# One core, a diffusion block with 16 experts: expert weights loaded in pairs of units, the last down matrix by column blocks, residual gates spread by transposes

## The chip, the cores and the metric

The kernel runs on one core of one Trainium2 chip, in fp32. The metric is the device time of one execution in microseconds (us), shown as the median of three runs. One of its executions was profiled; its rows are read further down.

## The reference

What is computed, cut to what matters here (512 latent tokens and 256 context tokens of 1024 channels, one layer):

```python
def ec_moe(h, w_r, w_g, w_u, w_d):
    cap = EC_CAPACITY_FACTOR * l_ // N_EXPERTS        # 64 tokens for each of 16 experts
    affinity = jax.nn.softmax((h @ w_r).astype(jnp.float32), axis=-1)
    gate, idx = lax.top_k(jnp.swapaxes(affinity, 1, 2), cap)
    xs = jax.vmap(lambda hb, ib: hb[ib])(h, idx)
    hid = jax.nn.silu(jnp.einsum('becd,edf->becf', xs, w_g)) * jnp.einsum('becd,edf->becf', xs, w_u)
    ye = jnp.einsum('becf,efd->becd', hid, w_d) * gate[..., None].astype(h.dtype)
...
        sh1, sc1, gt1, sh2, sc2, gt2 = adaln(c, w_ada[layer], b_ada[layer])
...
        h_lat = modulate(rms_norm(x, g_mix[layer]), sh1, sc1)
        u_l, q_l, v_l, gf_l, gb_l, g_l = split_proj(h_lat @ w_in[layer], lb)
...
        mix_l = jnp.concatenate([fourier_mix(u_l, w_fourier[layer]), rec_l], axis=-1) @ w_out[layer]
        x = x + gt1 * mix_l
...
        x = x + gt2 * ec_moe(modulate(rms_norm(x, g_ffn[layer]), sh2, sc2), w_router[layer],
                             w_exp_gate[layer], w_exp_up[layer], w_exp_down[layer])
    return rms_norm(x, g_final)
```

The experts' inner width is 2816. Their weights (gate, up and down, 16 x 3 x 1024 x 2816 floats) are 553 MB, nearly all that the kernel reads.

## The kernel before, in words

**Front.** The modulation vectors (shift, scale and residual gate, "ada") are a product of one row with `w_ada`. The class `AdaGroup` makes the last 4 x 1024 of them in two groups: `step` loads 1 MB of `w_ada` (L378, on SP) and VectorE multiplies and adds (L383, L385); `finish` adds over partitions on TensorE (L398), adds the bias on VectorE (`adag`, L400) and transposes (`adagT`, L403). Both `brow`, the bias, and `adag` live in two buffers with the tag `gcc`, which the function `ctx_states` takes over right behind for the scan states of the context (memset on POOL, L544; scans on DVE, L549 and L551; transposes on PE, L558). The residual gates `gt1b` and `gt2b` are the same row on every partition: a broadcast DMA reads the one partition row of `adag` 128 times (64 times), from ACT's queue, L589 and L615, two DMAs each.

Around this the input projection runs in segments of 512 columns (`ff`, `fb`, `v`, `g`, `u`, four steps each): a step's weights (512 KB, `fb1r` for step 1 of `fb`, L133, on SP) are split in a high part by ACT (`fb1wh`, L304) and a low part by POOL (`fb1wl`, L309), and TensorE multiplies three times (L145 to L147). The order of instructions on PE, DVE, ACT, POOL and SP is written by hand there (a manual schedule), and each engine works its list off in order. The gates of a finished segment go through ACT (L526, L532) and DVE. Then come heads, Fourier part, output projection and routing, a chain of computation up to about 370 us.

**Experts.** A matrix comes in 8 units of 128 x 2816 floats (1408 KB), one DMA each, all on SP's queue. Units lie in a ring of 13 equal areas: `slot()` names the next, `load_slot` (L1349) loads a unit in it when the area's last reader is done, and `load_ahead` (L1354) loads the first 13, and a fourteenth, `first`, in the memory of the hidden rows. A unit of the gate and up matrices is 128 rows of 11264 B that follow one another in memory; of the down matrix it is 128 runs of 11264 B that lie 45056 B apart. TensorE takes the units one by one: `up()` for gate (g) and up (u) (L1403), then `dn` (L1455); then `cb` (L1464) adds the expert's rows to `acc_x` on DVE (L1467). A DMA also needs one of eight completion lanes: a DMA waits for the one eight before it.

**The last expert** goes down in five column blocks (three of 256 columns, two of 128). `down_last` loads them by 22 DMAs (L1496) with runs of 1024 B or 512 B, and multiplies (`dq`, L1500); `combine_last` adds and normalises (`cq`, L1516), and out go four DMAs.

Of the kernel before, what the change touches and what calls it, by code (L numbers as in the profile page):

```python
# [30 lines left out]
NSLOT_L = 7  # L31
NSLOT_R = 6
# [19 lines left out]
# columns of the packed small operands  # L52
# [8 lines left out]
# and of its matrices  # L61
# [4 lines left out]
# columns of the packed shape constants  # L66
# [16 lines left out]
def hybrid_kernel(ctx: ExitStack, tc, x, ctxt, small, const, pos, w_ada, b_ada, w_in, w_out,  # L83
                  wg, wu, wd, out):
# [12 lines left out]
    # ------------------------------------------------------------------ memory that stays  # L97
# [25 lines left out]
    # ------------------------------------------------------------------ loads, in the order of use  # L123
# [52 lines left out]
    class AdaFirst:  # L176
        """Shift and scale of the mixer for channel blocks 2n and 2n+1."""

        def __init__(self, n):
            self.n = n  # L180
            if n % 2 == 0:
                # the memory of the values and of the context's gates
                w = p1b.tile([P, 2, 4, 256], F32, tag="v", name=f"adaw{n}_v")
                self.w = [w[:, 0], w[:, 1]] + [pc.tile([P, 4, 256], F32, tag=f"fctx{d}", name=f"adaw{n}_{d}")
                                               for d in range(2)]
            else:
                self.w = [wst.tile([P, 4, 256], F32, tag="wh" if t % 2 else "wl", bufs=SB, name=f"adaw{n}_{t}")
                          for t in range(4)]
            for t in range(4):
                # half of the rows of both halves of the sum  # L190
# [92 lines left out]
    # ------------------------------------------------------------------ input projection  # L283
    class Segment:
        """Columns col..col+512 of the projection, four steps of 256 channels each."""
# [10 lines left out]
        def split(self, kk, a, high=None, low=None):  # L296
            """High and low parts of half a tile."""
# [16 lines left out]
        def units(self, kk):  # L314
            """One step, in units of one 128x128 block of weights against all its tokens."""
# [33 lines left out]
            if kk in self.by_bank:  # L349
                # bank after bank: the last finish, and the next's first are needed, one by one  # L350
# [16 lines left out]
    class AdaGroup:  # L367
        """Columns g*2048..(g+1)*2048 of the modulation of the latent stream."""
# [4 lines left out]
        def step(self, k):  # L373
# [6 lines left out]
            # the products per channel of the sum; the tensor engine adds over the partitions  # L380
# [7 lines left out]
        def finish(self):  # L388
# [15 lines left out]
            return row, raw(tp[:], 0, [[32, 4], [P, 4]])  # L404
# [13 lines left out]
    # columns that add the partial sums  # L418
# [88 lines left out]
    # the gates, per head: forward, backward, queries  # L507
# [42 lines left out]
            # minus the decayed keys  # L550
# [72 lines left out]
    class Filler:  # L623
        """Work without close dependences, to be issued between the steps of the heads.

        What waits for a unit's matmuls is issued behind the next unit's.
        """
# [17 lines left out]
        def take(self, n):  # L645
            """Issues units; returns the tensor engine's time, negative where nothing should follow at once."""
# [22 lines left out]
    # the table of the function that the gate needs, loaded ahead  # L669
# [27 lines left out]
    # ------------------------------------------------------------------ HGRN2 heads  # L697
# [8 lines left out]
    def head_init(h):  # L706
        f, q = fq[:, h, 0:2, :], fq[:, h, 2, :]
        # slots: keys forward, queries backward, queries forward, keys backward
# [229 lines left out]
    def after_u():  # L938
        u_sb = p1b.tile([P, NH, S], F32, tag="u", name="u_sb")

        def wo_step(k, n):
# [51 lines left out]
        def positions(g):  # L993
# [10 lines left out]
            def evict():  # L1004
                # positions 0 and 256 of the cosines; even frequencies stand first
# [93 lines left out]
    class Steps:  # L1099
        """A generator with the tensor engine's time of each step."""  # L1100
# [19 lines left out]
    def fill_to(t, n=99):  # L1120
        """Issues units until the tensor engine has t us of work, n at most."""
# [57 lines left out]
    # ------------------------------------------------------------------ routing  # L1179
# [31 lines left out]
    # nothing, above the least, equal to it  # L1211
# [45 lines left out]
    def top(n):  # L1257
        """The CAP largest values of a row of candidates, in order."""
# [364 lines left out]
```

## Time and profile before

| | |
|---|---|
| median of 3 runs | 1672.88 us (1670.42 to 1674.8) |
| span of the profiled execution | 1668.7 us, 4.2 us under the median of the runs |
| PE, DVE, ACT, POOL busy | 92%, 24%, 15%, 10% |
| DMA packets, bytes | 91448, 608.37 MB |
| chain that ended last | DMA 48%, PE 41%, DVE 5%, ACT 2% |

The span runs from the first instruction to the last of the profiled execution; its own time is this span and the little around it, and the median of the runs stands 4.2 us above it. A busy PE share is not one of PE at its peak. The chain is followed back from the last instruction, at each step to what released it.

### The profile page before, as it was taken

How to read it: one execution, taken by the hardware profiler on the slowest of the kernel's cores; microseconds unless marked ns; L12 is line 12 of the kernel's file. 1: busy time of each engine (PE TensorE's matmuls, PEld its weight loads, DVE VectorE, ACT ScalarE, POOL GpSimd, SP SyncE). 2: the span in 40 equal slices, each digit the busy share in tenths (PEclk: the TensorE clock that was granted, in tenths of full speed). 3: DMA queues.
4: the chain of work that ended last, by engine and by line, in shares of the span. 5: the costliest groups of instructions: out<-in, count | busy, mean ns of one | idle time of the engine just before them, and what ended most of it. 6: DMA issues, size and time to landing. Idle time of an engine off the chain costs nothing.

```text
span 1668.7 us, 19918 instructions
## 1 busy us (share of the span) xinstructions
PE 1529.1 (92%) x8519; PEld 753.1 (45%) x8519; DVE 399.8 (24%) x754; ACT 255.9 (15%) x578; POOL 164.8 (10%) x153
## 2 busy tenths in 40 slices
PE   9978998989999999999898989988988899889897
PEld 6766776874443334343433343334333433243335
DVE  4855678370201010201011001100110111011103
ACT  4512456331000001000100010001000100010002
POOL 2623547400000000000000000000000000000002
PEclk9999999999999989999999998999999989999899
DMA  9785211859999999999999999999999999999998
GB/s 346 283 218 136 77 59 58 334 215 357 422 425 423 424 423 423 423 424 423 424 423 424 424 424 424 423 424 424 423 424 423 423 424 423 424 424 423 424 384 257
DMA packets 91448, 608.37 MB, mean 365 GB/s; under 512 B 8152, under 2 KB 30424, under 8 KB 41184
## 3 DMA queue, kind: packets, MB, share of 16 engines
q1 hardware_dynamic: 90480, 605.21, 88.6%
q10 hardware_dynamic: 880, 1.89, 1.5%
q8 instruction: 67, 1.10, 0.3%
q14 instruction: 21, 0.17, 0.0%
HBM read 604.18 MB, written 2.10 MB: 363 GB/s over the span
## 4 chain that ended last, share of the span: by engine, by line
DMA 48%; PE 41%; DVE 5%; ACT 2%; issue 1%; POOL 1%; SPq 0%; POOLq 0%; DVEq 0%; ACTq 0%
DMA uw<-in_wu_dram 18%; DMA gw<-in_wg_dram 15%; DMA dw<-in_wd_dram 12%; PE dn L1455 9%; PE g L1403 7%; PE u L1403 6%; PE gp L1375 4%; PE cb L1464 3%; DMA fb1r<-in_w_in_dram 1%; DMA adabuf<-in_w_ada_dram 1%; ACT xst L1377 1%; DVE X L795 1%; PE op L146 1%; PE op L145 1%; PE op L147 1%
## 5 line engine op out<-in xcount | busy, mean ns | idle before, releaser
L1455 PE MATMUL dn<-dw,hid 128*64 128x512 f32 (+1 forms) x1440 | 315.9, 562 | 9.0 <-DMA dw<-in_wd_dram 9.0
L1403 PE MATMUL u<-uw,xst 128*64 128x512 f32 (+1 forms) x1464 | 298.1, 559 | 23.4 <-DMA uw<-in_wu_dram 23.3
L1403 PE MATMUL g<-gw,xst 128*64 128x512 f32 (+1 forms) x1440 | 300.3, 569 | 0.0
L1403 PEld LDWEIGHTS u<-uw,xst 128*64 128x64 f32 x1464 | 102.7, 137 | 216.0 <-issue 165.1
L1455 PEld LDWEIGHTS dn<-dw,hid 128*64 128x64 f32 x1440 | 113.9, 136 | 168.1 <-issue 126.5
L1403 PEld LDWEIGHTS g<-gw,xst 128*64 128x64 f32 x1440 | 102.7, 139 | 187.0 <-issue 181.6
L1429 DVE TENSOR_TENSOR hid<-u,hid 128x512 f32<-128x512 f32 (+1 forms) x48 | 30.3, 647 | 538.5 <-PE u L1403 522.6
L1464 PE MATMUL cb<-ye,oht 64*128 64x512 f32 x240 | 108.9, 742 | 26.6 <-DVE acc_x L1467 15.6
L1415 ACT ACTIVATE hid<-g 128x512 f32<-128x512 f32 (+1 forms) x48 | 26.7, 561 | 655.2 <-PE g L1403 654.5
L1473 POOL COPY gt2f<-gt2b 64x512 f32<-64x512 f32 x2 | 1.2, 606 | 1265.8 <-DVE hid L1429 1265.8
L1375 PE MATMUL gp<-oh,xn 128*128 128x128 f32 x512 | 84.0, 294 | 23.3 <-ACT xst L1377 23.1
L1375 PEld LDWEIGHTS gp<-oh,xn 128*128 128x128 f32 x512 | 65.0, 190 | 74.5 <-issue 40.0
L1467 DVE TENSOR_TENSOR acc_x<-cb,acc_x 128x512 f32<-128x512 f32 x120 | 78.6, 688 | 57.6 <-PE cb L1464 57.6
L1377 ACT ACTIVATE xst<-gp,sh,a 128x128 f32<-128x128 f32 x64 | 29.3, 457 | 335.2 <-PE gp L1375 178.9
L1464 PEld LDWEIGHTS cb<-ye,oht 64*128 64x128 f32 x240 | 35.3, 206 | 97.2 <-DVE acc_x L1467 73.0
L1459 DVE TENSOR_TENSOR ye<-dn,gt2b 128x512 f32<-128x512 f32 x15 | 10.4, 692 | 214.9 <-PE dn L1455 214.9
L1437 ACT COPY hid<-hT 128x512 f32<-128x512 f32 (+1 forms) x48 | 24.8, 549 | 170.2 <-PE hT L1435 170.2
L1385 DVE TENSOR_TENSOR oh<-iota,posm 128x512 f32<-128x512 f32 x8 | 5.5, 692 | 182.8 <-PE gp L1375 182.7
L385 DVE SCALAR_TENSOR_TENSOR adaacc<-adabuf,cs,adaacc 128x1024 f32<-128x1024 f32 x28 | 44.3, 1642 | 5.1 <-DMA adabuf<-in_w_ada_dram 5.1
L1419 DVE TENSOR_SCALAR ohg<-iota,posm,aff 128x128 f32<-128x128 f32 x64 | 17.9, 343 | 103.2 <-PE ohT L1424 103.2
L1435 PE MATMUL hT<-ident,hid 128*128 128x128 f32 x176 | 29.3, 300 | 7.7 <-DVE hid L1429 5.9
L1435 PEld LDWEIGHTS hT<-ident,hid 128*128 128x128 f32 x176 | 23.9, 212 | 16.0 <-DVE hid L1429 11.6
(602 smaller groups left out, 1530.6 us busy)
## 6 DMA issues: line engine op xcount, KB each, us to landing
uw<-in_wu_dram SPq DMA_DIRECT2D x122, 1408.0 KB, 27.1
dw<-in_wd_dram SPq DMA_DIRECT2D x120, 1408.0 KB, 27.1
gw<-in_wg_dram SPq DMA_DIRECT2D x120, 1408.0 KB, 27.1
adabuf<-in_w_ada_dram SPq DMA_DIRECT2D x16, 1024.0 KB, 6.4
gw0a<-in_wg_dram SPq DMA_DIRECT2D x7, 1408.0 KB, 15.3
uw0a<-in_wu_dram SPq DMA_DIRECT2D x6, 1408.0 KB, 12.3
adaw<-in_w_ada_dram SPq DMA_DIRECT2D x24, 256.0 KB, 7.6
dw<-in_wd_dram SPq DMA_DIRECT2D x6, 768.0 KB, 13.9
```

The lines of the kernel that those rows point to most:

```text
L385: nv.scalar_tensor_tensor(self.acc[:, a], w[:, a], cs[:, k, :1], self.acc[:, a], op0=ALU.mult, op1=ALU.add)
L1375: nt.matmul(gather.gp[:, o:o + P], lhsT=xn[:, i, k * P:(k + 1) * P], rhs=oh[:, i].rearrange("p a j -> p (a j)"), start=(i == 0), stop=(i = ...
L1377: ns.activation(xst[:, k].rearrange("p a j -> p (a j)"), gather.gp[:, o:o + P], AF.Identity, bias=sh2[:, k:k + 1], scale=a2[:, k:k + 1])
L1403: nt.matmul(b[i][64 * hf:64 * hf + 64, :n], lhsT=xst[:, k, e % 2, :], rhs=t[:, hf * HALF + c0:hf * HALF + c0 + n], start=(k == 0), stop=(k ...
L1415: ns.activation(hid[:, c0:c0 + n], gb[i][:, :n], AF.Silu)
L1419: nv.tensor_scalar(ohg[:, i], iota[:, None, :].to_broadcast([P, 2, CAP]), posm[:, i, e:e + 1], aff[:, i, e:e + 1], op0=ALU.is_equal, op1=A ...
L1429: nv.tensor_tensor(hid[:, c0:c0 + n], ub[i][:, :n], hid[:, c0:c0 + n], op=ALU.mult)
L1435: nt.transpose(tp[:, (r - r0) * P:(r - r0 + 1) * P], hid.rearrange("p (f r) -> p r f", r=NROW)[:, r, :], ident)
L1437: ns.copy(hidT[:, r0:r0 + n].rearrange("p r j -> p (r j)"), tp[:, :n * P])
L1455: nt.matmul(db[64 * dh:64 * dh + 64, c0:c0 + n], lhsT=hidT[:, r, 64 * ih:64 * ih + 64], rhs=t[:, o:o + n], start=(ih == 0 and r == 0), sto ...
L1464: nt.matmul(cb, lhsT=oht[hs, i * P:(i + 1) * P], rhs=ye[hs, :], start=True, stop=True, tile_position=(64 * dh, 0))
L1467: nv.tensor_tensor(acc_x[:, i, ds_], cb, acc_x[:, i, ds_], op=ALU.add)
```

## The change

Three parts.

1. **Pairs.** The ring of 13 areas becomes six tiles of two areas each, and one spare area: `area(n)` hands out one area, or two that lie side by side. The table `BURST` says, for each expert's gate, up and down matrix, how many units one DMA loads: for expert 0 and the gate and up matrix of expert 1 single units, on the same 13 areas in the same order as before; from expert 1's down matrix on pairs, which no longer use the spare area. A pair is one DMA of 128 rows of 22528 B. For this the host lays the gate and up matrices out by partition (`wg`, `wu` as [expert, partition, 8 x 2816]), so that a partition's two units follow one another; a partition's row is then 90112 B from the next. The down matrix has its runs side by side already. There are 168 such pairs (4 + 13 x 12 + 8).
2. **Last down matrix.** The host lays it out by column blocks (`wd_last`), so that each of the 22 DMAs has one run per partition, of 6144 B to 1536 B, in place of several of 1024 B or 512 B.
3. **Gates.** The two broadcasts by DMA (L589, L615) go. DVE copies the gate's 8 columns out of `adagT` (`gt1c`, `gt2c`); for each half `spread` makes four transposes of a column that is repeated 128 times (`gt1s`, `gt2s`), which gives the row on every partition in a PSUM bank, and ACT copies it to `gt1b` (`gt2b`).

```diff
-NSLOT_L = 7
-NSLOT_R = 6
+PAIRS_L = 3
+PAIRS_R = 3
+
+BURST = [(1, 1, 1), (1, 1, 2)] + [(2, 2, 2)] * 13 + [(2, 2, 1)]
...
-    arow1, atp = ag1.finish()
+    def spread(cols, j, name):
+        tp = bank("m", name)
+        for i in range(4):
+            nt.transpose(tp[:, i * P:(i + 1) * P], cols[:, 4 * j + i:4 * j + i + 1].to_broadcast([P, P]), ident)
+        return tp
+
+    atp = ag1.finish()
     sh2 = pz.tile([P, NK], F32, name="sh2")
+    gt1c = pc.tile([P, NK], F32, tag="gtc", bufs=2, name="gt1c")
+    nv.tensor_copy(gt1c.rearrange("p (j i) -> p j i", j=2), atp[:, 0:2, :])
     nv.tensor_copy(sh2.rearrange("p (j i) -> p j i", j=2), atp[:, 2:4, :])
     for j in range(2):
-        src = arow1[32 * j:32 * j + 1, :]
-        ns.dma_start(gt1b[:, j * 512:(j + 1) * 512],
-                     bass.AP(src.tensor, src.offset, [list(src.ap[0]), [0, P], [1, 512]]))
+        ns.copy(gt1b[:, j * 512:(j + 1) * 512], spread(gt1c, j, f"gt1s{j}"))
...
     for j in range(2):
-        src = arow2[64 + 32 * j:65 + 32 * j, :]
-        ns.dma_start(gt2b[64 * j:64 * j + 64, :],
-                     bass.AP(src.tensor, src.offset, [list(src.ap[0]), [0, 64], [1, 512]]))
+        ns.copy(gt2b[64 * j:64 * j + 64, :], spread(gt2c, j, f"gt2s{j}")[64 * j:64 * j + 64, :])
...
+    spare = wl_pool.tile([P, DE], F32, name="wl_spare")
+    pairs = [(wl_pool if i < PAIRS_L else wr_pool).tile([P, 2 * DE], F32, name=f"w{i}")
+             for i in range(PAIRS_L + PAIRS_R)]
+    NU = 2 * len(pairs)
+    at, singles = [0], [True]
+    def area(n):
+        if singles[0] and n == 1:
+            u = at[0] % (NU + 1)
+            at[0] += 1
+            return spare if u == 0 else pairs[(u - 1) // 2][:, (u - 1) % 2 * DE:((u - 1) % 2 + 1) * DE]
+        if singles[0]:
+            assert at[0] % (NU + 1) == 0
+            singles[0], at[0] = False, 0
+        u = at[0] % NU
+        assert u % n == 0
+        at[0] += n
+        return pairs[u // 2][:, u % 2 * DE:(u % 2 + n) * DE]
+    def load_unit(w, e, u):
+        key = (w, e, u)
+        if key not in ahead:
+            n = BURST[e]["gud".index(w)]
+            t = area(n)
+            if w == "d":
+                nc.sync.dma_start(t, wds[e, u // 4, :, u % 4 * DE:(u % 4 + n) * DE])
+            else:
+                nc.sync.dma_start(t, {"g": wg, "u": wu}[w][e, :, u * DE:(u + n) * DE])
+            for i in range(n):
+                ahead[w, e, u + i] = t[:, i * DE:(i + 1) * DE]
+        return ahead.pop(key)
...
+            o, src = (ih % nh) * NROW * w, (2 * c0 + ih * w) * NROW
             for r0, r1 in ((0, 4), (4, 8), (8, NROW)) if n == 4 else ((0, 6), (6, NROW)):
-                nc.sync.dma_start(t[:, ih % nh, r0:r1], wdq[:, ih, r0:r1, c0:c0 + w])
+                nc.sync.dma_start(unit[:, o + r0 * w:o + r1 * w], wd_last[:, src + r0 * w:src + r1 * w])
```

Where it moves instructions. On PE, around the first transposes of the modulation (`adagT`), in the third part of segment `ff`, before:

```order
382 L403 MATMUL adagT_962<-ident,adag_955 128x128 x4
383 L146 MATMUL ff_l_747<-hlA,ff3wl 128x512
384 L147 MATMUL ff_l_747<-hlA,ff3wh 128x512
385 L145 MATMUL ff_l_748<-hlA,ff3wh 128x512
386 L146 MATMUL ff_l_748<-hlA,ff3wl 128x512
387 L147 MATMUL ff_l_748<-hlA,ff3wh 128x512
388 L145 MATMUL ff_l_748<-hlA,ff3wh 128x512
```

and of the change:

```order
382 L406 MATMUL adagT_962<-ident,adag_955 128x128 x4
383 L149 MATMUL ff_l_747<-hlA,ff3wl 128x512
384 L150 MATMUL ff_l_747<-hlA,ff3wh 128x512
385 L148 MATMUL ff_l_748<-hlA,ff3wh 128x512
386 L149 MATMUL ff_l_748<-hlA,ff3wl 128x512
387 L150 MATMUL ff_l_748<-hlA,ff3wh 128x512
388 L592 MATMUL gt1s_971<-ident,gt1c 128x128 x4
```

The eight transposes of `gt1s` stand between the matmuls of `ff`, in two lots of four five rows apart; those of `gt2s` stand likewise between the matmuls of `v`.

On SP, in the expert phase, a stretch of expert 2's list before (a unit each; the bracket names the completion lane and the engine that must have read the area):

```order
154 L1349 DMA uw_0_4356<-in_wu_dram 128x2816 [waits DMAHW3_49,PE_49]
155 L1349 DMA uw_1_4364<-in_wu_dram 128x2816 [waits DMAHW4_49,PE_49]
156 L1349 DMA uw_2_4372<-in_wu_dram 128x2816 [waits DMAHW5_49,PE_49]
157 L1349 DMA uw_3_4380<-in_wu_dram 128x2816 [waits DMAHW6_49,PE_49]
158 L1349 DMA uw_4_4388<-in_wu_dram 128x2816 [waits DMAHW7_49,PE_49]
```

and one of the change, a pair each:

```order
144 L1379 DMA w_3673<-in_wg_dram 128x5632 [waits DMAHW7_49,PE_49]
145 L1379 DMA w_3674<-in_wg_dram 128x5632 [waits DMAHW0_49,PE_49]
146 L1379 DMA w_3675<-in_wu_dram 128x5632 [waits DMAHW1_49,PE_49]
147 L1379 DMA w_3676<-in_wu_dram 128x5632 [waits DMAHW2_49,PE_49]
148 L1379 DMA w_3677<-in_wu_dram 128x5632 [waits DMAHW3_49,PE_49]
```

The sequence of matrices is the same, with half the DMAs, each twice as long; six tiles (`w_3673` to `w_3678`) come round.

## Rows read from the trace of the kernel before

**Rows 1.** The page: bytes moved in 40 slices of the span, and the packets.

```profile
GB/s 346 283 218 136 77 59 58 334 215 357 422 425 423 424 423 423 423 424 423 424 423 424 424 424 424 423 424 424 423 424 423 423 424 423 424 424 423 424 384 257
DMA packets 91448, 608.37 MB, mean 365 GB/s; under 512 B 8152, under 2 KB 30424, under 8 KB 41184
```

**Rows 2.** Windows: stretch, length, busy us by engine, PE clock, DMA share, GB/s.

```profile
85.56:93.90 8.34, 8.34 (x50) 7.29 (x48) 7.51 (x4) 0.00 (x0) 5.61 (x3) 1.00 0.46 164
102.00:115.00 13.00, 8.88 (x54) 7.69 (x52) 3.59 (x5) 0.60 (x1) 0.00 (x0) 1.00 0.98 58
103.86:150.20 46.34, 37.75 (x219) 33.43 (x218) 26.18 (x30) 10.10 (x18) 14.32 (x10) 0.93 0.77 209
700.00:1560.00 860.00, 790.90 (x3743) 308.32 (x3741) 99.78 (x177) 53.89 (x106) 0.00 (x0) 0.99 1.01 424
1634.00:1640.00 6.00, 6.00 (x43) 4.02 (x40) 1.38 (x2) 2.04 (x8) 2.39 (x2) 1.00 1.09 349
```

**Rows 3.** The chain that ended last, in order of time: start, length, what.

```profile
720.22 26.00 DMA dw<-in_wd_dram
746.27 27.11 DMA gw<-in_wg_dram
...
1594.24 27.37 DMA uw<-in_wu_dram
```

**Rows 4.** DMA issues: queue, count, KB each, median us from issue to landing.

```profile
uw<-in_wu_dram SPq DMA_DIRECT2D x122, 1408.0 KB, 27.1
dw<-in_wd_dram SPq DMA_DIRECT2D x120, 1408.0 KB, 27.1
...
gt1b<-adag ACTq DMA_DIRECT2D x2, 256.0 KB, 13.3
...
wo3r<-in_w_out_dram SPq DMA_DIRECT2D x1, 512.0 KB, 3.3
```

**Rows 5.** The chain of the stretch 50 to 320 us.

```profile
94.39 23.32 DMA fb1r<-in_w_in_dram
...
153.30 10.69 DMA gt2b<-adag
```

**Rows 6.** Timeline of POOL: start, length, what, and the idle time before.

```profile
117.90 0.10 POOL L544 MEMSET gcc<- 128x2 f32 x1 [21.39 <-DMA gt1b<-adag]
...
164.13 0.10 POOL L544 MEMSET gcc<- 128x2 f32 x1 [11.23 <-DMA gt2b<-adag]
```

**Rows 7.** Timeline of ACT.

```profile
98.51 0.60 ACT L532 ACTIVATE fq<-ff_l 128x512 f32<-128x512 f32 x1 [0.78 <-PE ff_l L147]
```

**Rows 8.** Timeline of PE.

```profile
96.02 0.60 PE L403 MATMUL adagT<-ident,adag 128*128 128x128 f32 x4
...
119.48 0.58 PE L145 MATMUL fb_c<-hctx_h,fb0wh 128*128 128x256 f32 x1 [8.59 <-ACT fctx L526]
...
165.88 0.80 PE L147 MATMUL v_l<-v1wl,hlB 128*128 128x512 f32 x1 [7.53 <-POOL v1wl L309]
```

**Rows 9.** Timeline of DVE.

```profile
153.96 0.14 DVE L610 SCALAR_TENSOR_TENSOR a<-adagT,sm 128x8 f32<-128x8 f32 x1
...
164.09 2.29 DVE L549 TENSOR_TENSOR_SCAN gcc<-fctx,zero 128x255 f32<-128x255 f32 x2 [9.24 <-DMA gt2b<-adag]
```

**Rows 10.** Waits of SP's queue: us in total, times, longest.

```profile
SPq L1349 <- PE g L1403: 164.0, 61, 13.2
```

**Rows 11.** Timeline of SP, then line 1349's DMAs issued from 536 to 552 us.

```profile
522.10 21.68 SPq L1349 DMA_DIRECT2D uw<-in_wu_dram  x6
...
DMA to landing us min/median/max: 12.1/12.6/13.1
```

**Rows 12.** Timeline of PE at expert 2, and at the last u unit.

```profile
536.10 7.31 PE L1403 MATMUL g<-gw,xst 128*64 128x512 f32 x36
...
1621.66 2.58 PE L1403 MATMUL u<-uw,xst 128*64 128x512 f32 x12 [0.81 <-DMA uw<-in_wu_dram]
```

**Rows 13.** Waits of PE: us in total, times, longest.

```profile
PE dq L1500 <- DMA dw<-in_wd_dram: 0.5, 2, 0.3
```

More of the change, by code (lines that the diff above doesn't have):

```diff
@@ L30 @@
 NROW = HALF // P
-NSLOT_L = 7
-NSLOT_R = 6
+PAIRS_L = 3
+PAIRS_R = 3
+BURST = [(1, 1, 1), (1, 1, 2)] + [(2, 2, 2)] * 13 + [(2, 2, 1)]
+BLOCKS = ((0, 256), (256, 256), (512, 256), (768, 128), (896, 128))
 ADA_AT = (1, 4)
@@ L83, in hybrid_kernel @@
 def hybrid_kernel(ctx: ExitStack, tc, x, ctxt, small, const, pos, w_ada, b_ada, w_in, w_out,
-                  wg, wu, wd, out):
+                  wg, wu, wd, wd_last, out):
     nc = tc.nc
@@ L403, in finish @@
                 nt.transpose(tp[:, i * P:(i + 1) * P], row[:, i * P:(i + 1) * P], ident)
-            return row, raw(tp[:], 0, [[32, 4], [P, 4]])
+            return raw(tp[:], 0, [[32, 4], [P, 4]])
     sq = Segment("q", 512, False, False)
@@ L607, in hybrid_kernel @@
         pass
-    arow2, atp = ag2.finish()
+    atp = ag2.finish()
     a2 = pz.tile([P, NK], F32, name="a2")
+    gt2c = pc.tile([P, NK], F32, tag="gtc", bufs=2, name="gt2c")
+    nv.tensor_copy(gt2c.rearrange("p (j i) -> p j i", j=2), atp[:, 2:4, :])
     nv.scalar_tensor_tensor(a2.rearrange("p (j i) -> p j i", j=2), atp[:, 0:2, :], 1.0,
@@ L1332, in hybrid_kernel @@
     wr_pool = tc.alloc_tile_pool(name="wr", bufs=1, side="right", reuse_waits="tile")
-    nslot = NSLOT_L + NSLOT_R
-    cnt = [0]
-    def slot(name):
-        i = cnt[0] % nslot
-        cnt[0] += 1
-        return (wl_pool if i < NSLOT_L else wr_pool).tile([P, DE], F32, tag=f"w{i}", name=name)
-    ahead = {}
-    def load_slot(src, name):
-        if name in ahead:
-            return ahead.pop(name)
-        t = slot(name)
-        nc.sync.dma_start(t, src)
-        return t
-    def load_ahead(w, nm, k, t=None):
-        t = t or slot(f"{nm}w0a_{k}")
-        nc.sync.dma_start(t, w[0, k * P:(k + 1) * P, :])
-        ahead[f"{nm}w0_{k}"] = t
+    spare = wl_pool.tile([P, DE], F32, name="wl_spare")
@@ new lines, in hybrid_kernel @@
+    wds = wd.rearrange("e (h p r) d -> e h p (r d)", h=2, p=P)
+    def load_unit(w, e, u):
[10 more added lines that the diff above has]
+        return ahead.pop(key)
@@ L1357, in hybrid_kernel, with load_ahead @@
+    def load_ahead(w, u, t=None):
+        if t is None:
+            t = area(1)
+        nc.sync.dma_start(t, {"g": wg, "u": wu}[w][0, :, u * DE:(u + 1) * DE])
+        ahead[w, 0, u] = t
     for k in range(NK - 1):
-        load_ahead(wg, "g", k)
-    for k in range(nslot - NK + 1):
-        load_ahead(wu, "u", k)
+        load_ahead("g", k)
+    for k in range(NU + 1 - NK + 1):
+        load_ahead("u", k)
     pe = tc.alloc_tile_pool(name="pe", bufs=1, side="right", reuse_waits="tile")
-    load_ahead(wg, "g", NK - 1, pe.tile([P, DE], F32, tag="hid", name="first"))
+    load_ahead("g", NK - 1, pe.tile([P, DE], F32, tag="hid", name="first"))
@@ L1391, in hybrid_kernel, with up @@
                     gather(xst, oh, e, k)
-        def up(w, name, first=False):
-            b = [bank("acc", f"{name}{e}_{i}") for i in range(3)]
+        def up(w, first=False):
+            b = [bank("acc", f"{w}{e}_{i}") for i in range(3)]
             if first:
@@ L1399, in up @@
                     gather(xst, oh, e, k + 1)
-                t = load_slot(w[e, k * P:(k + 1) * P, :], f"{name}w{e}_{k}")
+                t = load_unit(w, e, k)
                 for i, (c0, n) in enumerate(CH):
@@ L1410, in hybrid_kernel @@
         hid, hidT = hids[:, :HALF], hids[:, HALF:].rearrange("p (r j) -> p r j", j=P)
-        gb = up(wg, "g", e == 0)
+        gb = up("g", e == 0)
         if e == 0:
@@ L1426, in hybrid_kernel @@
         nv.tensor_copy(oht, tp)
-        ub = up(wu, "u")
+        ub = up("u")
         for i, (c0, n) in enumerate(CH):
@@ L1440, in hybrid_kernel @@
         db = bank("z", f"dn{e}")
-        wde = wd[e].rearrange("(h p r) d -> h p (r d)", h=2, p=P)
         for s8 in range(8):
             ih, s = divmod(s8, 4)
-            t = load_slot(wde[ih, :, s * DE:(s + 1) * DE], f"dw{e}_{s8}")
+            t = load_unit("d", e, s8)
             pos_ = s * DE
@@ L1484, in hybrid_kernel @@
     junkf = pe.tile([P, S], F32, tag="ohg", name="junkf")
-    wdq = wd[NE - 1].rearrange("(h p r) d -> p h r d", h=2, p=P)
-    BLOCKS = ((0, 256), (256, 256), (512, 256), (768, 128), (896, 128))
     def down_last(n):
@@ L1493, in down_last @@
             if ih % nh == 0:
-                t = slot(f"dw{NE - 1}_{n}_{ih}").rearrange("p (h r c) -> p h r c", h=nh, c=w)
+                unit = area(1)
+                t = unit.rearrange("p (h r c) -> p h r c", h=nh, c=w)
+            o, src = (ih % nh) * NROW * w, (2 * c0 + ih * w) * NROW
             for r0, r1 in ((0, 4), (4, 8), (8, NROW)) if n == 4 else ((0, 6), (6, NROW)):
-                nc.sync.dma_start(t[:, ih % nh, r0:r1], wdq[:, ih, r0:r1, c0:c0 + w])
+                nc.sync.dma_start(unit[:, o + r0 * w:o + r1 * w], wd_last[:, src + r0 * w:src + r1 * w])
             for r in range(NROW):
@@ L1602 @@
     posf, cst = _shape_constants()
+    by_partition = lambda w: w.reshape(NE, NK, P, DE).transpose(0, 2, 1, 3).reshape(NE, P, NK * DE)
+    last = a["w_exp_down"].reshape(NE, DE, D)[NE - 1].reshape(2, P, NROW, D).transpose(1, 0, 2, 3)
     ins = {
@@ L1607 @@
         "w_in": a["w_in"].reshape(D, -1), "w_out": a["w_out"].reshape(D, D),
-        "wg": a["w_exp_gate"].reshape(NE, D, DE), "wu": a["w_exp_up"].reshape(NE, D, DE),
-        "wd": a["w_exp_down"].reshape(NE, DE, D),
+        "wg": by_partition(a["w_exp_gate"]), "wu": by_partition(a["w_exp_up"]),
+        "wd": a["w_exp_down"].reshape(NE, DE, D)[:NE - 1],
+        "wd_last": np.concatenate([last[..., c0:c0 + w].reshape(P, -1) for c0, w in BLOCKS], axis=1),
     }
```

## The prediction

> **What bounds the kernel now.** The page's slices come first: the rate is 422 to 425 GB/s in every slice from the eleventh to the thirty-eighth, and uneven before [rows 1]. So there are two stages. The windows tell what limits each: from 700 to 1560 us the DMA engines are busy all the time (share 1.01) at 424 GB/s, while TensorE works 790.9 of 860 us [rows 2]. The chain of waits says the same: from 720 us on it is one DMA after another, 27.1 us each, the time that a unit needs from issue to landing with seven others ahead of it [rows 3, 4]. There the time is bytes over rate, and an engine's work matters only where it holds back a load.
>
> Before that stage the reader should look at the chain of the stretch 50 to 320 us. Two DMAs stand out: `fb1r` for 23.32 us, and `gt2b` for 10.69 us [rows 5]. `fb1r` is a weight load of 512 KB like `wo3r`, which took 3.3 us [rows 4]. It is slow because of what lies in front of it: from 102 to 115 us the DMA engines were busy for 0.98 of the time, yet moved 58 GB/s [rows 2]. That is the broadcast `gt1b`, 128 reads of one partition's row, 13.3 us from issue to landing [rows 4]. POOL meanwhile stood 21.39 us at a memset, since the scan buffer `gcc` is the memory that the broadcast reads, and 11.23 us for `gt2b` [rows 6].
>
> **The gates by transposes.** Removed are four broadcast DMAs on ACT's queue. Added are four lots of four transposes on PE, 0.60 us a lot by `adagT` x4; four copies of up to 128x512 on ACT, 0.60 us each [rows 7]; two copies of 128x8 on DVE, 0.14 us each by an operation of that size [rows 9]. ACT and DVE have room: 10.10 and 26.18 us busy in the 46.34 us of segment `fb` [rows 2]; were that cover gone, it would be 2.4 and 0.3 us. PE is on the path there, so its 0.60 us count, 1.2 us for each gate [rows 8].
>
> The first wait: segment `fb` takes 46.34 us for 37.75 us of PE work at a clock of 0.93, while a step of `ff` of the same size ran at 1.00 in 8.34 us without a gap [rows 2]. The gap is the 8.59 us in which `fb_c` waits for ACT, which waits for `fb1r`; right behind it the matmuls are slow [rows 8]. If `fb1r` lands some 7 us after its issue, both go: 8.6 us of idle time plus up to 7% of 37.75 us (2.6 us), less 1.2 us, which is 7.4 to 10 us. I take 8.5. Late next is `fb2r`, issued at 101.47 us behind the same broadcast; it should come early for the same reason.
>
> The second wait: DVE stands 9.24 us before the scans [rows 9] and PE 7.53 us before `v_l` [rows 8], the chain has 10.69 us [rows 5]. With the DMA gone `gcc` is free when the transposes have read `adag`, so 9.2 to 10.7 us go, less 1.2 us on PE, and partly less where DVE has its scans to do anyway. I take 9. What follows up to about 370 us is a chain of computation and moves as a whole, the prefetch of the first units with it. Front: **-17.5 us**. Bounds: -23 (both waits with all that the clock loses) and -9 (one wait comes back as another).
>
> **Pairs, the rate.** The trace has no row of 22528 B, so its price is bounded. A row of 11264 B costs 11264 x 16 / 424 = 425 ns of an engine, and one of 1024 B costs 1024 x 16 / 349 = 46.9 ns [rows 2]. The line through both has 0.0369 ns per byte and 9.1 ns per row. A pair saves 8 rows on each of 16 engines, 73 ns; 168 pairs save **12 us**. The upper end is 18 us, if the shares of 1.01 and 1.09 are multiplied in (429 and 51 ns, 13 ns a row); the lower end is nothing, if 424 GB/s is a ceiling of its own. I take the line, since the 11264 B row is the nearest and lies on it by construction. TensorE still has room: 69 us in the 860.
>
> The page "DMA: Bandwidth & Descriptors" of the Trainium skill (section "Measured") gives 425 GB/s for a load of 16 MB, called 97% of the peak. Were that all one core can draw, this part would give nothing and the sum would be 1661 us; the trace's 424 GB/s agrees with either reading, and no run here has a longer row.
>
> **Pairs, the ring.** The ring has 12 areas for 13, and an area comes free only when both units of its pair are read. Where does that bite? At expert 2, where PE starts at 536.10 us [rows 12] far behind the loads. The six `uw` loads before 546 us are issued in 21.68 us, paced by PE, and landing then takes 12.1 us at the least seen [rows 11] in place of 27.1. PE takes 2.4 us a unit and the DMA 3.4 us (27.1 / 8), so going back from there each earlier unit lands 1.0 us sooner after its issue: about 9 us for the first of them that waited for expert 2. An empty queue would need 3.3 us for 512 KB [rows 4] and 2.2 us for the other 896 KB, 5.5 us. The margin is 3.5 us; one area less costs 3.4 us of it and the second unit of the pair 2.4 us. So the queue runs dry, once, for 2.3 us by this count, up to 4.5 if a start out of an empty queue takes longer. I take **+3.5 us** (0 to 6). Behind it PE catches up by some 9 us an expert, and from 720 us on it waits for the loads, not they for it [rows 3]. SP waits 61 times for an area that `g` reads, 13.2 us at the longest [rows 10]; that costs nothing while transfers are queued ahead of it, which from 720 us on are 27 us worth. The six tiles hold 12 x 3.4 = 41 us of loads.
>
> **The tail.** The last `u` unit lands at 1594.24 + 27.37 = 1621.6 us, and PE, which had waited, does it in 2.58 us [rows 3, 12]. With a pair two units are left, +2.4 us. From there to the end PE computes: for the column blocks it waits 0.5 us in all [rows 13]. So their longer runs, which make 1 KB rows at 349 GB/s [rows 2] into rows at nearly full rate, save at most 0.5 us. Tail: **+2 us** (-0.5 to +3).
>
> **Sum.** -17.5 - 12 + 3.5 + 2 = -24 us on the span of 1668.7 us, 1644.7 us. The median of the runs is 4.2 us above the span, so **1649 us**.
>
> **Rivals.**
> - A, the rate is a ceiling: pairs move 424 GB/s too. For it: the rate is flat to 0.7% over 28 slices [rows 1]. Against: the line from the short rows. -17.5 + 3.5 + 2 = -12, 1661 us. Chance 0.18.
> - B, the front gives half: a weight load or the `w_ada` loads of the second group, behind one another on SP, are late next, or the heads wait for something else. For it: the 1 MB loads of `w_ada` stand between `fb1r` and `fb3r` on SP's queue. Against: segment `fb` drew 209 GB/s over its whole length with the broadcast inside, 424 is there. -9 - 12 + 3.5 + 2 = -15.5, 1657 us. Chance 0.13.
> - A and B together: -3.5 us, 1669 us. Chance 0.03.
> - C, slower: the ring runs dry at every expert, not only at the second. Each pair is released 2.4 us late, and at each expert PE stops loading on the ring while it gathers and combines. At 3.5 us for each of 13 experts it is 45 us for 3.5: 1690 us; it decides from 2.1 us an expert. Against: from 720 us PE is the one that waits. Chance 0.04.
> - D, slower: rows of 22528 B that lie 90112 B apart draw less from memory. It would touch the 112 pairs of gate and up, some 760 us, so a loss of 3.2% of the rate cancels the whole gain, and 5% gives 1687 us, the gain of their rows included as nothing. Against: `dw`, whose rows lie 45056 B apart, lands in the same 27.1 us as `uw`, whose rows follow one another [rows 4]. Chance 0.03. The page "DMA: Bandwidth & Descriptors" of the Trainium skill (section "Latency and other measured facts") states that copies slow down where a partition's rows lie a large power of two apart (half the rate at 4 MiB); 90112 B is none, and no run here shows that pitch.
>
> The rest, 0.59, is the forecast. What 0.3% (5 us) can't tell from no change is A with B. Faster: 0.59 + 0.18 + 0.13 = 0.90; no change 0.03; slower 0.07. The range takes in the forecast's own bounds, A and B, and leaves C and D out: 1636 us (front -22, pairs -15, ring and tail 0) to 1664 us (A with the ring at its upper bound).
>
> **What the changed profile should show.** `fb1r` landing in under 10 us and no DMA in the waits of `gcc`; the segment `fb` in 37 to 39 us at a clock near 1.00; the first gather of expert 0 some 17 us sooner. In the expert phase 427 to 428 GB/s (A: 424; D: less) and one dip of the DMA share of 2 to 5 us near 520 us (C: at every expert). The page should count 91448 - 168 x 128 (pairs) - 384 (broadcasts) - (14080 - 2816) (last down matrix) = 58,296 packets. PE with two units behind the last landing, and about 49 us from there to the end. The prediction fails if the windows of the pairs show another rate than 424 to 429 GB/s, or if the front moves by less than 9 us.

## The result and the profile after

The changed kernel takes 1645.53 us (median of 4 runs, 1644.8 to 1646.65) against 1673.07 us (1670.42 to 1674.8, 4 runs): a ratio of 0.984, 95% interval 0.9826 to 0.9854. The forecast was 1649 us in 1636 to 1664. The profiled execution has a span of 1642.7 us, 26.0 us less. The forecast added 4.2 us to go from the span to the median, as before the change; here the median stands 2.8 us above the span.

The page after, slices and packets, against [rows 1]:

```profile
GB/s 345 282 282 96 65 91 69 325 271 400 425 428 356 429 429 429 429 429 429 429 428 429 429 429 429 429 429 429 428 430 429 429 427 429 429 429 429 429 422 212
DMA packets 55543, 607.56 MB, mean 370 GB/s; under 512 B 5401, under 2 KB 13849, under 8 KB 26785
```

From the twelfth slice to the thirty-eighth the rate is 427 to 430 GB/s where it was 422 to 425, with one hole: the thirteenth slice has 356.

The windows, against [rows 2] (stretch, length, busy us by engine, PE clock, DMA share, GB/s). The first takes in segment `fb`, 0.8 us of `ff` before it and 1.0 us of `v` behind it; the second holds the hole:

```profile
103.60:141.20 37.60, 37.60 (x232) 33.13 (x234) 26.43 (x31) 9.97 (x19) 12.32 (x9) 1.00 0.55 210
500.00:540.00 40.00, 38.25 (x164) 13.75 (x162) 7.75 (x14) 1.69 (x3) 0.00 (x0) 0.91 0.85 353
700.00:1540.00 840.00, 776.05 (x3667) 310.40 (x3664) 99.34 (x173) 52.24 (x103) 0.00 (x0) 0.97 1.00 429
```

In the window of `fb` before, PE was busy for 37.75 of 46.34 us; now it has no gap, at a clock of 1.00. From the first matmul of `fb` to the first of `v` it was 46.1 us (103.86 to 149.97) and is 35.7 us (104.43 to 140.17), and `v` starts 9.8 us sooner. Before and after:

```profile
149.97 0.48 PE L145 MATMUL v_l<-v0wh,hlB 128*128 128x512 f32 x1
...
140.17 0.48 PE L148 MATMUL v_l<-v0wh,hlB 128*128 128x512 f32 x1
```

POOL's timeline, against [rows 6], shows the second wait: the memsets of the scan buffer wait for an addition and for transposes, and no DMA is named any more.

```profile
96.33 0.49 POOL L547 MEMSET gcc<- 128x2 f32 x1 [0.17 <-PE adagT L406]
...
143.00 0.10 POOL L547 MEMSET gcc<- 128x2 f32 x1 [12.47 <-DVE adag L403]
143.75 0.10 POOL L547 MEMSET gcc<- 128x2 f32 x1 [0.65 <-PE adagT L406]
```

The weights that the broadcast had held up, in the DMA issues (last column: us from issue to landing, 23.32 us in the chain before [rows 5]):

```profile
fb1r<-in_w_in_dram SPq DMA_DIRECT2D x1, 512.0 KB, 7.8
```

The rest of the bill is read from PE's timeline at two places: the first gather `gp` of expert 0, and the last wait for `u` weights. Before:

```profile
371.76 2.02 PE L1375 MATMUL gp<-oh,xn 128*128 128x128 f32 x16 [0.17 <-DVE oh L1385]
```

After:

```profile
352.46 1.80 PE L1408 MATMUL gp<-oh,xn 128*128 128x128 f32 x14 [0.17 <-DVE oh L1418]
...
1594.29 4.95 PE L1436 MATMUL u<-w,xst 128*64 128x512 f32 x24 [1.81 <-DMA w<-in_wu_dram]
```

| part | before | after | change | forecast |
|---|---|---|---|---|
| front, to the first gather | 371.76 | 352.46 | -19.3 | -17.5 |
| from there to the last `u` landing that PE waits for (before: 1621.66 [rows 12]) | 1249.9 | 1241.8 | -8.1 | -12 + 3.5 |
| from there to the end | 47.0 | 48.4 | +1.4 | +2 |
| span | 1668.7 | 1642.7 | -26.0 | -24 |

The middle row holds two things, what the pairs' rate brought and what a hole in the loads took back. From 500 to 540 us the DMA engines moved 353 GB/s; at 429 that is a loss of 40 x 76 / 429 = 7.1 us, which would leave 15 us for the rate. A kernel without the hole (pairs later, below) parts the two better: its middle row is 1237.3 us (354.44 to 1591.69), 12.7 us less than before with 156 pairs, so 13.6 us for 168, and 5.5 us are left for the hole. The hole is therefore 5.5 to 7.1 us, the rate 13.6 to 15.

In the hole SP waits for TensorE: from 495 to 540 us its longest wait for an area is one of 15.4 us, for `g` of expert 2 (us in total, times, longest).

```profile
SPq L1379 <- PE g L1436: 15.4, 1, 15.4
```

### The profile page after: what moved, and what is told of

The parts are those of the page before. It is cut to its first block, busy times and chain, and to the rows that moved or that the text cites. A ratio compares the mean times of both kernels' runs of the same rounds, so it can differ in the third digit from the quotient of the medians.

```text
span 1642.7 us, 19617 instructions
## 1 busy us (share of the span) xinstructions
PE 1519.7 (93%) x8535; PEld 757.9 (46%) x8535; DVE 401.3 (24%) x756; ACT 257.9 (16%) x582; POOL 163.8 (10%) x153
## 2 busy tenths in 40 slices
DMA packets 55543, 607.56 MB, mean 370 GB/s; under 512 B 5401, under 2 KB 13849, under 8 KB 26785
## 4 chain that ended last, share of the span: by engine, by line
PE 71%; DMA 19%; DVE 6%; ACT 3%; issue 1%; POOL 0%; SPq 0%; DVEq 0%; POOLq 0%; ACTq 0%
PE g L1436 16%; PE dn L1487 15%; PE u L1436 11%; DMA w<-in_wu_dram 10%; DMA w<-in_wd_dram 7%; PE cb L1496 6%; PE gp L1408 4%; ACT xst L1410 1%; DVE acc_x L1499 1%; PE dq L1533 1%; DVE X L806 1%; PE hT L1468 1%; PE op L148 1%; PE op L149 1%; PE op L150 1%
## 5 line engine op out<-in xcount | busy, mean ns | idle before, releaser
L1436 PE MATMUL u<-w,xst 128*64 128x512 f32 x1524 | 305.6, 558 | 18.2 <-DMA w<-in_wu_dram 18.2
L1436 PE MATMUL g<-w,xst 128*64 128x512 f32 x1500 | 316.8, 572 | 0.0
L1487 PE MATMUL dn<-w,hid 128*64 128x512 f32 (+1 forms) x1440 | 308.3, 560 | 8.5 <-DMA w<-in_wd_dram 8.5
L1436 PEld LDWEIGHTS u<-w,xst 128*64 128x64 f32 x1524 | 110.0, 137 | 210.7 <-issue 177.8
L1487 PEld LDWEIGHTS dn<-w,hid 128*64 128x64 f32 x1440 | 119.9, 137 | 170.6 <-issue 135.2
L1436 PEld LDWEIGHTS g<-w,xst 128*64 128x64 f32 x1500 | 106.8, 140 | 197.4 <-issue 192.8
L1496 PE MATMUL cb<-ye,oht 64*128 64x512 f32 x240 | 115.4, 789 | 26.0 <-DVE acc_x L1499 15.0
L1408 PE MATMUL gp<-oh,xn 128*128 128x128 f32 x512 | 80.4, 291 | 23.8 <-ACT xst L1410 23.6
L1468 PEld LDWEIGHTS hT<-ident,hid 128*128 128x128 f32 x176 | 23.9, 212 | 16.0 <-DVE hid L1462 11.5
```

Of the source, the lines that this page charges most:

```text
L1408: nt.matmul(gather.gp[:, o:o + P], lhsT=xn[:, i, k * P:(k + 1) * P], rhs=oh[:, i].rearrange("p a j -> p (a j)"), start=(i == 0), stop=(i = ...
L1436: nt.matmul(b[i][64 * hf:64 * hf + 64, :n], lhsT=xst[:, k, e % 2, :], rhs=t[:, hf * HALF + c0:hf * HALF + c0 + n], start=(k == 0), stop=(k ...
L1468: nt.transpose(tp[:, (r - r0) * P:(r - r0 + 1) * P], hid.rearrange("p (f r) -> p r f", r=NROW)[:, r, :], ident)
L1487: nt.matmul(db[64 * dh:64 * dh + 64, c0:c0 + n], lhsT=hidT[:, r, 64 * ih:64 * ih + 64], rhs=t[:, o:o + n], start=(ih == 0 and r == 0), sto ...
L1496: nt.matmul(cb, lhsT=oht[hs, i * P:(i + 1) * P], rhs=ye[hs, :], start=True, stop=True, tile_position=(64 * dh, 0))
```

## The experiments

Eight kernels. Their medians and ratios, with 95% intervals, are against the kernel before, measured beside them. Where a run is set against the changed kernel, two medians of different times are compared; the kernel before had medians of 1672.1 to 1673.1 us at these times.

**The gates alone.** The kernel before with part 3 of the change and nothing else.

```diff
-        ns.dma_start(gt1b[:, j * 512:(j + 1) * 512],
-                     bass.AP(src.tensor, src.offset, [list(src.ap[0]), [0, P], [1, 512]]))
+        ns.copy(gt1b[:, j * 512:(j + 1) * 512], spread(gt1c, j, f"gt1s{j}"))
...
-        ns.dma_start(gt2b[64 * j:64 * j + 64, :],
-                     bass.AP(src.tensor, src.offset, [list(src.ap[0]), [0, 64], [1, 512]]))
+        ns.copy(gt2b[64 * j:64 * j + 64, :], spread(gt2c, j, f"gt2s{j}")[64 * j:64 * j + 64, :])
```

> The kernel before with the third part of the change alone (residual gates by transposes, expert loads as before). Theory: the two broadcasts explain the whole front, so the time is 17 to 18 us below before (about 1655 us), the weights fb1r land in under 10 us and the expert phase still runs at 424 GB/s. Rival (half): a load behind fb1r is late in its place and only 9 us are won, 1664 us. Rival (the front's gain needs the rest of the change): no gain, 1673 us.

Measured: 1652.62 us, 0.9881 (0.9866 to 0.9895), 19.7 us less by the medians, 16.5 by the spans of the two profiles, and the first gather starts 16.4 us sooner (355.40 us). `fb1r` lands in 7.9 us, and the expert phase stays at 424 GB/s:

```profile
700.00:1540.00 840.00, 770.21 (x3601) 296.30 (x3598) 99.01 (x173) 52.20 (x103) 0.00 (x0) 0.98 1.01 424
```

So the gates carry most of the whole gain, and they need nothing else of the change.

**One gate back.** The changed kernel with `gt2b` by DMA again.

```diff
-    atp = ag2.finish()
+    arow2, atp = ag2.finish()
...
-        ns.copy(gt2b[64 * j:64 * j + 64, :], spread(gt2c, j, f"gt2s{j}")[64 * j:64 * j + 64, :])
+        src = arow2[64 + 32 * j:65 + 32 * j, :]
+        ns.dma_start(gt2b[64 * j:64 * j + 64, :],
+                     bass.AP(src.tensor, src.offset, [list(src.ap[0]), [0, 64], [1, 512]]))
```

> The changed kernel with the second gate (gt2b) by broadcast DMA again, the first by transposes. Theory: the two waits are independent, so the wait of the scans for the DMA is back and costs 8 to 10 us: 1654 us, and the last single unit of expert 1 lands 8 to 10 us later than in the changed kernel. Rival: the front has slack once the first wait is gone, and less than 3 us come back: 1648 us.

Measured: 1653.1 us, 0.9887 (0.9874 to 0.9901), 7.6 us above the changed kernel. DVE's wait is back as it was [rows 9], at an earlier time:

```profile
155.11 2.29 DVE L552 TENSOR_TENSOR_SCAN gcc<-fctx,zero 128x255 f32<-128x255 f32 x2 [9.35 <-DMA gt2b<-adag]
```

The first gather starts at 363.01 us. In the six kernels that spread both gates by transposes it starts between 352.46 and 355.40, so the second gate is worth 7.6 to 10.6 us; the first is worth the 8.8 us by which 363.01 is earlier than 371.76. The waits add up: neither hid behind the other.

**The last down matrix alone**, in the kernel before.

```diff
-            for r0, r1 in ((0, 4), (4, 8), (8, NROW)) if n == 4 else ((0, 6), (6, NROW)):
-                nc.sync.dma_start(t[:, ih % nh, r0:r1], wdq[:, ih, r0:r1, c0:c0 + w])
+            o, src = (ih % nh) * NROW * w, (2 * c0 + ih * w) * NROW
+            for r0, r1 in ((0, 4), (4, 8), (8, NROW)) if n == 4 else ((0, 6), (6, NROW)):
+                nc.sync.dma_start(unit[:, o + r0 * w:o + r1 * w], wd_last[:, src + r0 * w:src + r1 * w])
```

> The kernel before with the second part alone (last down matrix by column blocks, 22 DMAs with one run per partition). Theory: TensorE sets the tail, so 0.5 us at most is won, 1672 to 1673 us. Rival: the short rows hold up the last up units, which are in flight beside them, and the tail wins 3 to 4 us, 1669 us.

Measured: 1671.15 us, 0.9991 (0.9982 to 1.0001). The DMA page has 80184 packets for 91448, and the interval of the time takes in no change. PE no longer waits for column blocks (0.5 us before [rows 13]). From the last wait for `u` weights to the end the profile has 46.1 us (1621.50 to 1667.6) for 47.0 before. Over the kernels whose last up matrix comes in single units, this stretch is 46.1 us in the three with the new layout and 46.7 to 47.2 in the three with the old one: some 0.6 to 1.1 us, a little more than the waits.

**Pairs of short rows.** The changed kernel with gate and up matrices in their old layout, so that a pair is one DMA of 256 rows of 11264 B.

```diff
-                nc.sync.dma_start(t, {"g": wg, "u": wu}[w][e, :, u * DE:(u + n) * DE])
+                nc.sync.dma_start(t.rearrange("p (n d) -> p n d", n=n), {"g": wg, "u": wu}[w][e, u * P:(u + n) * P, :]
+                                  .rearrange("(n p) d -> p n d", p=P))
```

> The changed kernel with the gate and up matrices in their old layout, so that a pair of these is one DMA of 256 rows of 11264 B (112 of the 168 pairs); the down matrices keep rows of 22528 B. Theory (a fixed cost per row): those pairs fall back to 424 GB/s, the down pairs stay at 429, and the time is 9 to 11 us above the changed kernel, 1655 us. Rival (a cost per DMA, halved by pairs whatever their rows): they stay at 429 GB/s, 1645 us. Rival (the wide pitch costs something): faster than the changed kernel.

Measured: 1650.81 us, 0.9871 (0.9852 to 0.9891), 5.3 us above the changed kernel; its four runs scatter more than the others', from 1648.83 to 1654.83. Within this one kernel the windows part the rows; in the first and third nearly all of what moved was down pairs with rows of 22528 B, in the second and fourth gate and up pairs with rows of 11264 B (the last of four down pairs went out at 863.48 us and landed 30.49 us later, in the chain that ended last; two experts on, one went out at 1026.87 and landed after 30.97):

```profile
868.00:886.00 18.00, 17.04 (x85) 7.87 (x81) 1.90 (x3) 1.55 (x3) 0.00 (x0) 1.00 1.00 428
897.00:930.00 33.00, 31.26 (x126) 11.02 (x124) 6.63 (x10) 0.34 (x1) 0.00 (x0) 0.90 1.01 423
1030.00:1048.00 18.00, 17.01 (x89) 7.02 (x87) 1.89 (x3) 1.55 (x3) 0.00 (x0) 1.00 1.00 428
1060.00:1090.00 30.00, 28.26 (x112) 10.03 (x110) 6.63 (x10) 0.00 (x0) 0.00 (x0) 0.89 1.01 424
```

The DMAs of both kinds are equally long, 2816 KB. So the rate goes by the length of a row, not by the number of DMAs, and the wide pitch costs nothing that shows. The time went up by less than the 9 to 11 us expected, and the hole at expert 2 is smaller here: 396 GB/s from 500 to 540 us instead of 353. Why it is smaller comes with the account of the ring below.

```profile
500.00:540.00 40.00, 38.25 (x162) 13.53 (x160) 7.74 (x14) 1.68 (x3) 0.00 (x0) 0.91 0.96 396
```

**Pairs later.** The changed kernel with single units on 13 areas up to expert 2's up matrix.

```diff
-BURST = [(1, 1, 1), (1, 1, 2)] + [(2, 2, 2)] * 13 + [(2, 2, 1)]
+BURST = [(1, 1, 1)] * 2 + [(1, 1, 2)] + [(2, 2, 2)] * 12 + [(2, 2, 1)]
...
-            assert at[0] % (NU + 1) == 0
-            singles[0], at[0] = False, 0
+            o = at[0] % (NU + 1)
+            assert o % 2 == 1
+            singles[0], at[0] = False, o - 1
```

> The changed kernel with single units on 13 areas up to expert 2's up matrix, pairs from its down matrix on (156 pairs for 168). Theory: the DMA engines ran dry for 6 us at expert 2 because 6 pair tiles are one area fewer and come free a unit later; with 13 areas there they do not, and 12 pairs at 0.1 us each are given back: 5 us below the changed kernel, about 1640.5 us, with no dip of the DMA share at 500 to 540 us. Rival: the dip belongs to TensorE being late at expert 2 or to the change of ring, and stays or moves to expert 3: no gain, 1645 us.

Measured: 1641.14 us, 0.9808 (0.9792 to 0.9824), 4.4 us below the changed kernel. The hole is gone, and did not move to another slice:

```profile
GB/s 346 269 275 117 66 80 59 348 257 385 424 423 424 430 429 429 429 429 429 429 428 429 428 429 429 429 429 430 428 430 428 429 427 427 429 429 428 430 419 201
```

**A ring of 12 areas in the kernel before.**

```diff
-NSLOT_R = 6
+NSLOT_R = 5
```

> The kernel before with a ring of 12 areas for 13, single units throughout. It parts the two causes of the dip at expert 2. Theory (margin of 3.5 us; an area fewer costs 3.4 us, the release of both units at once 2.4 us and more): the queue just about does not run dry, under 1 us, 1672 to 1674 us. Rival (the area alone makes the dip): 4 to 6 us slower with a dip of the DMA share near 545 us, 1677 to 1679 us.

Measured: 1675.46 us, 1.0019 (1.001 to 1.0028), 3.4 us slower, and no hole: 424 GB/s from 520 to 560 us. Between the two expectations, and it does not part the causes. With one area fewer, one unit fewer is loaded ahead, so the loads should be some 3.4 us later from the start and meet expert 2 with that much more queue left; the least time from issue to landing between 520 and 560 us is 13.7 us for 12.1 before, which fits. The price of an area would then have been paid early.

**Single units on 12 areas, where the pairs begin.** This parts what the run before could not.

```diff
-BURST = [(1, 1, 1), (1, 1, 2)] + [(2, 2, 2)] * 13 + [(2, 2, 1)]
+BURST = [(1, 1, 1)] * 16
...
             n = BURST[e]["gud".index(w)]
+            if (w, e, u) == ("d", 1, 0):
+                assert at[0] % (NU + 1) == 0
+                singles[0], at[0] = False, 0
             t = area(n)
```

> The changed kernel with single units throughout, but on the six pair tiles (12 areas, no spare) from expert 1's down matrix on, where the pairs begin in the changed kernel. It parts the area given up from the release of two units at once. Theory (both make the dip, which measured 7 us): with single releases 2.5 to 4 us of it stay, and the DMA engines show a dip of that length near expert 2's first matmul; the rate is 424 GB/s, which costs 14 us; the pair's 2.4 us at the end are won back: 1653 to 1656 us. Rival (the release of both units makes the dip alone): no dip, 1651 to 1652 us. Rival (the area alone): the dip stays at 6 to 7 us, 1658 us.

Measured: 1653.0 us, 0.989 (0.9873 to 0.9906), as the gates alone. There is no hole:

```profile
500.00:540.00 40.00, 38.07 (x175) 13.58 (x173) 8.68 (x18) 1.68 (x3) 0.00 (x0) 1.00 1.01 423
```

My theory falls: the area given up did not run the queue dry. It did take some of the queue: the shortest time from issue to landing behind expert 2's first `g` matmuls is 9.7 us here and 11.5 us in the kernel with the gates alone, which has 13 areas. SP's longest wait for `g` from 495 to 540 us is 10.3 us, for 15.4 with pairs. What differs with the pairs is in PE's timeline. Here, PE at expert 2's start:

```profile
515.48 7.31 PE L1439 MATMUL g<-w,xst 128*64 128x512 f32 x36
```

and in the changed kernel:

```profile
518.15 5.76 PE L1436 MATMUL g<-w,xst 128*64 128x512 f32 x24
```

An area that a pair needs comes free when 24 matmuls are done, at 518.15 + 5.76 = 523.9 us; that of a single unit after 12, at about 518.1 us (the first gather of the two kernels stands 1.5 us apart the other way, at 352.46 and 353.98). That is 5.8 us later, or 7.3 counted from the first gather; the hole lost 5.5 to 7.1 us.

**Both ends single.** Pairs later, as above, and the last up matrix in single units.

```diff
-BURST = [(1, 1, 1)] * 2 + [(1, 1, 2)] + [(2, 2, 2)] * 12 + [(2, 2, 1)]
+BURST = [(1, 1, 1)] * 2 + [(1, 1, 2)] + [(2, 2, 2)] * 12 + [(2, 1, 1)]
```

> The changed kernel with single units up to expert 2's up matrix, as in the run before, and single units also for the last up matrix (152 pairs). Theory: the dip at expert 2 is gone, and TensorE has one unit left behind the last landing and not two; that takes 1.5 to 2.4 us off the tail and gives back 0.3 us for four pairs: 1639 to 1640 us, the tail from the last landing to the end 46 to 47 us. Rival: the last units land no sooner, since the loads of the last down matrix move beside them, and the tail stays at 49 us: 1641 us.

Measured: 1639.37 us (1639.14 to 1640.81), 0.9804 (0.979 to 0.9817), 1.8 us below the median of the run with pairs at the end, whose runs overlap with these (1639.84 to 1642.29), and 6.2 us below the changed kernel: the lowest median here. PE has one unit behind the last landing:

```profile
1592.65 2.58 PE L1437 MATMUL u<-w,xst 128*64 128x512 f32 x12 [0.83 <-DMA w<-in_wu_dram]
```

From there to the end of the span, 1638.7 us, it is 46.1 us; the changed kernel has 48.4 and the run with pairs later 48.5. This stretch shows the gain more plainly than the medians do.

## Why the prediction was right, and which term was off

The terms were off by -1.8 us (front), -1.6 (rate), +2.0 (ring) and -0.6 (tail), taken from the bill with the hole at 5.5 us. They cancel in part, which helped the sum: -26.0 us of span for -24.

**The front, -17.5 forecast, -19.3 in the profile.** The chain of reasoning held at each step: the broadcast filled the DMA engines, `fb1r` waited behind it, ACT behind `fb1r`, PE behind ACT; and the scan buffer was held by the second broadcast. The first wait gave 9.8 us at the start of `v` for 8.5 forecast, since `fb` takes 35.7 us and not the 37 to 39 foretold. The second gate gave 7.6 to 10.6 us for 9. Of the six profiles with both gates spread this one has the earliest first gather; over the six the front moved by 16.4 to 19.3 us. Rival B, that one of the waits returns as another, is refuted by the gates alone and by one gate back.

**The rate, -12 forecast, 13.6 to 15 measured.** The line through rows of 1024 B and 11264 B foretold a gain per row, not a ceiling. 424 GB/s became 429 where 427 to 428 was expected. The 168 pairs hold 484.4 MB: 1142.5 us at 424 and 1129.2 at 429, so 13.3 us, or 80 ns a pair and 10 ns a row on each engine, for 9.1 by the line; the kernel without a hole gives 13.6. Rival A, 424 as a ceiling, is refuted; so is the figure of the Trainium skill read as one ("DMA: Bandwidth & Descriptors", section "Measured": 425 GB/s): the trace shows 429 on one core. Rival D, the pitch of 90112 B, is refuted by the short rows, which were slower without that pitch; this agrees with the page's section "Latency and other measured facts" of the Trainium skill, whose slow pitches are large powers of two. (D's price of 1687 us is the forecast and 38 us; with the gain of its rows taken as nothing, as it says, it would be some 8 us more.)

**The ring, +3.5 forecast, 5.5 to 7.1 measured.** This is the mis-sized term. Place and kind were right: once, at expert 2, and not later, against rival C. The size came from the step "one area less costs 3.4 us of it and the second unit of the pair 2.4 us". The area alone emptied nothing: single units on 12 areas had no hole, and by the landing times above it took 1.8 us of the queue and not 3.4. With a margin of 3.5 us the prediction's own count would have allowed that too; what it missed lies in the pair. The pair's area came free 7.3 us later than a single unit's, counted from the first gather, for the 2.4 us foretold. Some 3.1 us of it are the second unit (24 matmuls in 5.76 us, 12 in 2.6). The other 4.2 us are PE's later start on expert 2: its first `g` matmul comes 165.7 us after the first gather in the changed kernel and 161.5 with single units.

That later start goes with the clock. In the changed kernel's profile the clock fell twice while an expert's rows were added up (`cb`): with expert 0, from 428 to 434 us, and with expert 1, from 513 to 519 us. In windows of 1 us it is 0.50 to 0.51 there, the lower of its two levels (1.2 GHz). Just before, PE had waited 0.78 us for DVE twice, as it had with single units, where the clock stayed at 1.00. First the changed kernel, then single units on 12 areas, then short rows:

```profile
420.00:440.00 20.00, 19.04 (x65) 7.41 (x63) 6.63 (x10) 0.00 (x0) 0.00 (x0) 0.83 1.01 422
500.00:520.00 20.00, 18.25 (x64) 6.59 (x62) 6.63 (x10) 0.00 (x0) 0.00 (x0) 0.83 0.94 395
512.70 5.52 PE L1496 MATMUL cb<-ye,oht 64*128 64x512 f32 x8 [0.19 <-DVE acc_x L1499]
...
420.00:440.00 20.00, 18.85 (x80) 7.93 (x78) 6.45 (x10) 0.00 (x0) 0.00 (x0) 1.00 1.01 423
500.00:520.00 20.00, 18.07 (x75) 6.37 (x73) 7.56 (x14) 0.00 (x0) 0.00 (x0) 1.00 1.01 422
511.93 1.72 PE L1499 MATMUL cb<-ye,oht 64*128 64x512 f32 x4 [0.18 <-DVE acc_x L1502]
...
420.00:440.00 20.00, 18.86 (x80) 7.98 (x78) 6.45 (x10) 0.00 (x0) 0.00 (x0) 1.00 1.01 423
500.00:520.00 20.00, 18.25 (x62) 6.34 (x60) 6.63 (x10) 0.00 (x0) 0.00 (x0) 0.83 1.01 424
511.45 5.52 PE L1497 MATMUL cb<-ye,oht 64*128 64x512 f32 x8 [0.19 <-DVE acc_x L1500]
```

From the third `cb` lot of expert 1 to expert 2's first `g` matmul it is 5.45 us at the low clock (512.70 to 518.15) and 3.55 at the high one (511.93 to 515.48): 1.9 us. With short rows the clock fell only this second time, and `g` starts at 162.9. The 2.8 us from there to 165.7 go with the first fall; the kernel before, with 0.83 from 440 to 460 us, starts `g` 2.8 us later than the gates alone too (164.3 for 161.5). With one gate back the clock fell both times again, and `g` starts at 165.6. The pairs' other order of work, gathers and down matmuls in longer lots, cost PE nothing: with short rows the first `cb` of expert 1 comes 0.5 us sooner after the first gather than with single units (153.6 for 154.1).

The size of the hole follows: 7.1 us here, where the area comes free 171.4 us after the first gather; about 7 with one gate back, at 171.3; 3.1 us with short rows (40 x (429 - 396) / 429), at 168.7. By the medians of the run without a hole it is 5.4 us (4.4, and 1.0 for 12 pairs given up). How much the lower rate of the short rows adds to the difference was not tried apart. Nor was the case of pairs with no fall of the clock, so what the second unit alone would do to the queue stays open.

**The tail, +2 forecast, +1.4 measured.** A pair left PE two units, which cost 2.3 us (48.4 for 46.1 with single units at the end). The column blocks gave some 0.6 to 1.1 us back where 0.5 at most was expected; the time of the kernel with this part alone does not tell it from nothing.

**The packets, 58,296 forecast, 55,543 counted.** The difference of 2753 is 16 packets for each of the 168 DMAs that the pairs saved and the 4 broadcasts (2752): a DMA has 16 packets beside its rows, which the forecast left out. The gates alone show it too, with 448 packets less for 4 DMAs of 384 rows. For the pairs they cost nothing that shows, as the pairs of short rows tell: those saved them too, and ran at 423 to 424 GB/s.

## What to carry to other kernels

A broadcast by DMA out of one partition is paid by whatever stands behind it on the same DMA engines and by whoever takes over its source's memory; here eight transposes (1.2 us of TensorE) and two copies per gate freed some 8 to 10 us each time. Where a stream of loads is the bound, as here, longer rows were worth some 10 ns per row saved on each engine, and fewer DMAs with the same rows nothing. Larger pieces of a ring served best where the ring had slack: pairs in the middle, single units where the reader was furthest behind the loads and where little should be left after the last landing.

## What the runs showed of the hardware that I had not expected

- One core read 429 GB/s over 840 us with rows of 22528 B and 424 with rows of 11264 B, with DMAs of the same 2816 KB, and with a pitch of 90112 B for the longer rows. That is about 10 ns for a row on each engine, at rows as long as these.
- With the same program up to expert 1, the clock fell to 0.83 in a stretch of 20 us in one kernel's profile (420 to 440 us) and stayed at 1.00 in another's. Two such falls, 2.8 and 1.9 us of PE time, moved PE's start on expert 2 by 4.7 us in all, and with it the release of an area and the hole in the loads. What decides whether it falls stays open.
